# HGRN in a two-layer hybrid backbone: level 0 in one PSUM tile and one step with the product of each token with itself, and the output's products in one step

## The chip, the core and the metric

The kernel runs on one core of a Trainium2 chip. The metric is the time of one execution in device microseconds, as the median of several runs. Engines are named as the profile names them: PE is the matrix engine (PEld its weight loads), DVE the vector engine, ACT the scalar engine, POOL the GpSimd engine, SP the engine that issues most of the DMAs. Each engine takes its instructions in the order in which they were written into its queue, and waits for other engines through semaphores.

## What is computed

Two layers run over 640 tokens: 128 of context and 512 of a latent grid. Each layer projects its input to many columns, feeds four mixers with them, and merges the four results. The change is in the first mixer, HGRN2, a gated linear recurrence in both directions with 4 heads of width 128:

```python
def chunk_gla(q, k, v, log_g, s0):
    ...
    def step(S, inp):
        qc, kc, vc, gc = inp
        b = jnp.cumsum(gc, axis=2)
        diff = b[:, :, :, None, :] - b[:, :, None, :, :]
        decay = jnp.exp(jnp.where(causal[:, :, None], diff, -jnp.inf))
        attn = jnp.einsum('bhtd,bhsd,bhtsd->bhts', qc, kc, decay)
        o = (jnp.einsum('bhts,bhse->bhte', attn, vc)
             + jnp.einsum('bhtd,bhde->bhte', qc * jnp.exp(b), S))
        ...
```

The score of two tokens is their product, weakened by all gates between them. The kernel builds it by levels: level `lev` treats pairs of neighbouring blocks of 2 to the power `lev` tokens, so each pair of tokens gets its score at one level, and a token with itself (the "own" product) before level 0.

## The kernel before

Everything is held with channels on partitions and tokens along the free dimension. The input `h` is split into `h_hi` and `h_lo`, and each weight into `whi` and `wlo`, so a product takes three matmuls. One chunk of 128 projected columns (`zchunk`) has two halves of tokens, of 384 and 256 (`HALVES`), and each half 24 matmuls of L217 into one of two PSUM tiles `g`. A chunk's weights come by DMA, then ACT casts `whi` (L160), and DVE subtracts to get `wlo` (L161).

What is not a projection runs beside it in Python generators ("streams"). Before each half of a chunk the main program calls `tick()`. A stream that yields a number sleeps for that many ticks, so the code between two yields is a "step" that is written between two halves. `merge_chunk` has three ticks: two for the halves of its projection, and one before the 24 matmuls of L208 with the branch weights. The recorded program then goes through a scheduler of the language, which may put an instruction later in its engine's queue than the code does where it reckons with a wait, and sets the semaphores. It keeps track of whole tiles.

The streams that matter here:

- `hg_mix` (one for each head, two at a time at most): transposes of `v` (L514), the own product (L526) and its copy to `C` (L528), seven levels (keys `km` copied at L536, product L547, its part taken over into `C` at L549, keys, queries and gates brought on at L559 to L565), transposes of the keys (L574), states (L584), the output (L607, 13 products that PE runs as 26 instructions), its norm, and the transpose back (L620). Steps are `HG_WAIT` = 2 ticks apart, the first `HG_W0` = 3. All its PSUM tiles are `mx`, of which there are three, each two banks of 512 floats wide.
- `mods` (modulation of this layer's end and of the next layer, by DVE, ACT and POOL): 6 groups of products in layer 0 and 2 in layer 1. A group takes 14 ticks, and in 7 of them DVE (L405), ACT (L406) and POOL (L407) do one pass over 128x512 each; the sum at L410 ends it, and L417 takes the result out of PSUM. `mods` starts when the stream of head 2 has ended.
- `mla_mix` and `na_all`, the attention mixers. In `na_mix` a softmax is normed on POOL (`norm`, L929), and PE then transposes it (`TR`, L973).

In a layer the order is: the four heads' projections with the fourth mixer's, the merge of that mixer (8 `merge_chunk`s), the MLA, the merge of HGRN, neighbourhood attention, two more merges, and the output. `merge_chunk` takes its product out of PSUM on DVE (L1057 in the first merge, L1059 in the others), and the next projection needs that tile.

Of the kernel before, what the change touches and what calls it, by code (L numbers as in the profile page):

```python
# [13 lines left out]
ALU = mybir.AluOpType  # L14
# [4 lines left out]
T = 640  # L19
# [63 lines left out]
def ap_of(t, off, dims):  # L83
    base = t[:]
    return bass.AP(tensor=base.tensor, offset=base.offset + off, ap=[list(base.ap[0])] + [list(d) for d in dims])


class Build:
# [414 lines left out]
    def hg_mix(self, l, h, z, out):  # L503
        nc = self.nc
        G, RK, RQ, q, vT, sg = z
        S0 = self.u([128, 2, 128])
        nc.sync.dma_start(S0, self.I["S0"][l, h])
        ks = self.t()
        nc.vector.tensor_tensor(ks, RK[:, 0, :], RK[:, 1, :], ALU.add)
        yield HG_W0  # L510

        ps = self.mx()
        for j in range(5):
            nc.tensor.transpose(ps[:, j * 128:(j + 1) * 128], vT[:, j * 128:(j + 1) * 128], self.ident)  # L514
        v = self.t()
        nc.scalar.copy(v, ps[:, :T])


        halves = (slice(0, 64), slice(64, 128))
        five = lambda x: x[:, 0:320].rearrange("p (j t) -> p j t", j=5)  # L520

        ps = self.mx()
        for j in range(5):
            for i, r in enumerate(halves):
                sl = slice(j * 128 + 64 * i, j * 128 + 64 * i + 64)
                nc.tensor.matmul(ps[r, j * 64:(j + 1) * 64], ks[:, sl], q[:, sl], start=True, stop=True)  # L526
        C = self.t([128, 5, 64])
        nc.scalar.copy(C, five(ps))  # L528
        nc.vector.tensor_tensor(RQ[:, 0, :], q, G[:, 0, :], ALU.mult)
        nc.vector.tensor_tensor(RQ[:, 1, :], q, G[:, 1, :], ALU.mult)  # L530
        Tb, n = G, T
        for lev in range(7):
            B = 1 << lev
            np_ = T // (2 * B)
            km = self.t()
            nc.scalar.copy(km.rearrange("p (n u b) -> p n u b", u=2, b=B),  # L536
                           ap_of(RK, 0, [[2 * B, np_], [T + B, 2], [1, B]]))
            yield HG_WAIT
            ps = self.mx()
            for j in range(5):  # L540
                for i, r in enumerate(halves):
                    o = j * 128 + 64 * i
                    if B < 64:
                        x = ap_of(RQ, o, [[2 * B, 32 // B], [T + B, 2], [1, B]])
                    else:
                        x = RQ[:, 1 - i, j * 128 + 64 - 64 * i:j * 128 + 128 - 64 * i]
                    nc.tensor.matmul(ps[r, j * 64:(j + 1) * 64], km[:, o:o + 64], x, start=True, stop=True)  # L547
            if B < 64:
                nc.vector.copy_predicated(C, self.masks[:, lev:lev + 1, :].to_broadcast([128, 5, 64]), five(ps))  # L549
            else:  # L550

                A = self.t()
                Aj = A.rearrange("p (j t) -> p j t", j=5)
                for i, r in enumerate(halves):
                    nc.scalar.copy(Aj[r, :, 64 * i:64 * i + 64], C[r])
                    nc.scalar.copy(Aj[r, :, 64 - 64 * i:128 - 64 * i], five(ps)[r])

            kf = ap_of(RK, 0, [[2 * B, np_], [1, B]])
            nc.vector.tensor_tensor(kf, kf, ap_of(Tb, n + 1, [[2, np_], [0, B]]), ALU.mult)  # L559
            kb = ap_of(RK, T + B, [[2 * B, np_], [1, B]])  # L560
            nc.vector.tensor_tensor(kb, kb, ap_of(Tb, 0, [[2, np_], [0, B]]), ALU.mult)  # L561
            rq = ap_of(RQ, 0, [[2 * B, np_], [T + B, 2], [1, B]])
            nc.vector.tensor_tensor(rq, rq, ap_of(Tb, 1, [[2, np_], [n - 1, 2], [0, B]]), ALU.mult)
            T2 = self.t([128, 2, np_]) if lev == 0 else self.u([128, 2, np_])
            nc.vector.tensor_tensor(T2, ap_of(Tb, 0, [[n, 2], [2, np_]]), ap_of(Tb, 1, [[n, 2], [2, np_]]), ALU.mult)  # L565
            Tb, n = T2, np_
        yield HG_WAIT

        order = ((0, 1, 2, 3), (0, 4, 3, 2))
        ps = self.mx()  # L570
        for d in range(2):
            for i, j in enumerate(order[d]):
                o = (4 * d + i) * 128
                nc.tensor.transpose(ps[:, o:o + 128], RK[:, d, j * 128:(j + 1) * 128], self.ident)  # L574
        kt = [self.t([128, 4, 128]) for _ in range(2)]
        for d in range(2):
            nc.scalar.copy(kt[d], ps[:, 512 * d:512 * d + 512].rearrange("p (i t) -> p i t", i=4))
        yield HG_WAIT
        vv = lambda j: v[:, j * 128:(j + 1) * 128]
        ps = self.mx()  # L580
        for d in range(2):
            for i, j in enumerate(order[d]):
                o = (4 * d + i) * 128
                nc.tensor.matmul(ps[:, o:o + 128], kt[d][:, i, :], vv(j), start=True, stop=True)  # L584
        st = self.u([128, 2, 128])
        nc.scalar.copy(st, ps.rearrange("p (d i t) -> p d i t", d=2, i=4)[:, :, 0, :])
        nc.sync.dma_start(self.O["state"][l, h], st)
        S = [self.u([128, 3, 128]) for _ in range(2)]
        terms = {j: [(A[:, j * 128:(j + 1) * 128], vv(j))] for j in range(5)}
        for d in range(2):  # L590
            prev = S0[:, d, :]
            for i in range(1, 5):
                j = order[d][i] if i < 4 else (4, 1)[d]
                terms[j].append((RQ[:, 1 - d, j * 128:(j + 1) * 128], prev))
                if i < 4:
                    o = (4 * d + i) * 128
                    nc.vector.scalar_tensor_tensor(S[d][:, i - 1, :], prev, Tb[:, 1 - d, j:j + 1], ps[:, o:o + 128],
                                                   ALU.mult, ALU.add)
                    prev = S[d][:, i - 1, :]
        yield HG_WAIT  # L600

        ps = self.mx()
        for j in range(5):
            if j == 3:
                yield 1
            for i, (a, b) in enumerate(terms[j]):
                nc.tensor.matmul(ps[:, j * 128:(j + 1) * 128], a, b, start=(i == 0), stop=(i == len(terms[j]) - 1))  # L607
        sq = self.t()
        nc.scalar.activation(sq, ps[:, :T], AF.Square)
        ss = self.sm([128, 5])  # L610
        nc.vector.tensor_reduce(ss, sq.rearrange("p (j e) -> p j e", j=5), AX.X, ALU.add)
        r = self.sm([128, 5])
        self.rsqrt(r, ss, 5, 1.0 / 128, EPS)
        on = sq
        nc.vector.tensor_tensor(on.rearrange("p (j e) -> p j e", j=5), ps[:, :T].rearrange("p (j e) -> p j e", j=5),
                                r.unsqueeze(2).to_broadcast([128, 5, 128]), ALU.mult)
        yield HG_WAIT
        ps = self.mx()
        for j in range(5):
            nc.tensor.transpose(ps[:, j * 128:(j + 1) * 128], on[:, j * 128:(j + 1) * 128], self.ident)  # L620
        nc.vector.scalar_tensor_tensor(sg, ps[:, :T], self.vec("normg", l), sg, ALU.mult, ALU.mult)
        out[h] = sg
# [706 lines left out]
HG_WAIT = 2  # L1329
# [120 lines left out]
```

## Time and profile before

| what | value |
|---|---|
| runs | 2124.34 us median (2123.99 to 2128.66, three runs) |
| profiled execution | 2129.58 us, span 2127.5 us |
| PE busy | 2071.5 us (97%) |
| DVE, ACT, POOL busy | 1369.0 us (64%), 879.1 us (41%), 181.2 us (9%) |
| granted TensorE clock | 0.989 |

The profiled execution's own time is 2.1 us over its span. PE's busy time counts from an instruction's start to its end, and neighbouring matmuls overlap, so a time between two starts says more than a mean. [...]

### The profile page before, as it was taken

To read this page: it belongs to the slowest core of one execution; us is meant where nothing else is said; L and a number is where in the kernel's file an instruction comes from. 1 tells how busy PE (TensorE), PEld (TensorE's weight loads), DVE (VectorE), ACT (ScalarE), POOL (GpSimd) and SP (SyncE) were. 2 spreads that over 40 slices of the span, in tenths; PEclk is the share of its full clock that TensorE was granted. 3 is DMA by queue.
4 is the path that set the end of the run, shared out by engine and by line. 5 is a ranking of instruction groups with operands and counts; after the bars stand their busy time and mean duration, and the time that the engine had idled before them with its cause. 6 is when DMAs were issued, how large, how long until landed. Compare 5 with 4: busy or idle time off the path is not lost. (4 is left out here: it accounts for less than half of the span.)

```text
span 2127.5 us, 36907 instructions
## 1 busy us (share of the span) xinstructions
PE 2071.5 (97%) x15114; PEld 2013.0 (95%) x15114; DVE 1369.0 (64%) x2653; ACT 879.1 (41%) x1564; POOL 181.2 (9%) x156
## 2 busy tenths in 40 slices
PE   7999999999999999999999999999999999999997
PEld 4999999999999999999989999999999999999997
DVE  5677776568565667734487876873765546775456
ACT  4333334334445556523352333342443346663332
POOL 0000000111011133200010000010100002231000
PEclk9999999999999999999999999999999999999999
DMA  7222213344324411222432222143322212212251
GB/s 284 74 73 61 67 59 106 111 131 145 97 95 144 137 64 61 70 69 81 135 120 70 63 63 71 57 137 95 117 67 63 67 58 70 68 59 65 75 163 50
DMA packets 79849, 194.66 MB, mean 91 GB/s; under 512 B 9152, under 2 KB 22208, under 8 KB 79680
## 3 DMA queue, kind: packets, MB, share of 16 engines
q1 hardware_dynamic: 76656, 186.10, 27.4%
q10 hardware_dynamic: 3024, 6.20, 0.9%
q8 instruction: 119, 1.95, 0.4%
q14 instruction: 50, 0.41, 0.1%
HBM read 184.73 MB, written 7.54 MB: 90 GB/s over the span
## 5 line engine op out<-in xcount | busy, mean ns | idle before, releaser
L217 PE MATMUL g<-h_hi,whi 128*128 128x256 f32 (+1 forms) x2880 | 905.9, 315 | 16.6 <-DVE m L1057 7.0
L217 PE MATMUL g<-h_lo,whi 128*128 128x256 f32 (+1 forms) x2880 | 892.9, 310 | 0.6 <-DVE h_lo L1129 0.2
L217 PE MATMUL g<-h_hi,wlo 128*128 128x256 f32 (+1 forms) x2880 | 891.9, 310 | 0.6 <-DVE wlo L161 0.6
L217 PEld LDWEIGHTS g<-h_hi,whi 128*128 128x128 f32 x2880 | 548.1, 190 | 25.5 <-DVE m L1057 7.6
L217 PEld LDWEIGHTS g<-h_lo,whi 128*128 128x128 f32 x2880 | 548.7, 191 | 3.1 <-DVE h_lo L1129 1.6
L217 PEld LDWEIGHTS g<-h_hi,wlo 128*128 128x128 f32 x2880 | 548.1, 190 | 1.0 <-DVE wlo L161 1.0
L161 DVE TENSOR_TENSOR wlo<-wraw,whi 128x1024 fp32r<-128x1024 f32 (+1 forms) x258 | 284.1, 1101 | 281.7 <-ACT whi L160 279.5
L160 ACT CAST whi<-wraw 128x1024 fp32r<-128x1024 f32 (+1 forms) x258 | 242.8, 941 | 457.3 <-PE g L217 243.1
L208 PE MATMUL g<-t,whi 128*128 128x256 f32 (+1 forms) x1280 | 283.5, 311 | 0.7 <-ACT e L1044 0.7
L208 PEld LDWEIGHTS g<-t,whi 128*128 128x128 f32 x1280 | 214.2, 189 | 2.2 <-ACT e L1044 1.2
L208 PE MATMUL g<-t,wlo 128*128 128x384 f32 (+1 forms) x640 | 197.8, 309 | 0.0
L407 POOL TENSOR_TENSOR t<-t 128x512 f32<-128x512 f32 x56 | 82.2, 1468 | 1083.2 <-ACT t L406 1042.8
L929 POOL TENSOR_SCALAR u<-u,sm 128x320 f32<-128x320 f32 (+2 forms) x80 | 89.6, 1131 | 475.9 <-DVE sm L927 443.9
L208 PEld LDWEIGHTS g<-t,wlo 128*128 128x128 f32 x640 | 121.0, 189 | 0.0
L1044 ACT ACTIVATE e<-g,hbin 128x384 f32<-128x384 f32 (+1 forms) x128 | 67.0, 523 | 115.7 <-PE g L217 113.0
L260 ACT ACTIVATE e<-g,hbin 128x384 f32<-128x384 f32 x76 | 39.9, 525 | 97.7 <-PE g L217 80.3
L261 DVE TENSOR_SCALAR e<-g,vecs 128x384 f32<-128x384 f32 x76 | 41.3, 544 | 45.5 <-ACT e L260 45.2
L477 DVE RECIPROCAL s<-e 128x384 f32<-128x384 f32 (+1 forms) x32 | 68.8, 2149 | 0.7
L854 ACT ACTIVATE t<-mx,sm,rq 128x640 f32<-128x640 f32 (+1 forms) x40 | 31.9, 797 | 63.6 <-DVE sm L851 61.2
L536 ACT COPY t<-s 128x640 f32<-128x640 f32 x56 | 43.5, 780 | 30.4 <-DVE s L561 30.4
L405 DVE SCALAR_TENSOR_TENSOR t<-t,cf 128x512 f32<-128x512 f32 x56 | 52.7, 941 | 3.2 <-DMA t<-in_wada 1.6
L1059 DVE SCALAR_TENSOR_TENSOR e<-e,g 128x384 f32<-128x384 f32 x96 | 46.4, 484 | 12.9 <-PE g L208 12.3
(290 smaller groups left out, 2666.1 us busy)
## 6 DMA issues: line engine op xcount, KB each, us to landing
wraw<-in_win SPq DMA_DIRECT2D x184, 512.0 KB, 3.6
t<-in_wada SPq DMA_DIRECT2D x128, 256.0 KB, 4.3
wraw<-in_wbr SPq DMA_DIRECT2D x64, 256.0 KB, 2.6
wraw<-in_wout SPq DMA_DIRECT2D x20, 512.0 KB, 4.2
s<-in_wada SPq DMA_DIRECT2D x16, 512.0 KB, 7.6
s<-in_nabias SPq DMA_DIRECT2D x8, 640.0 KB, 4.9
m<-in_xT SPq DMA_DIRECT2D x8, 320.0 KB, 8.3
t<-in_xT ACTq DMA_DIRECT2D x8, 320.0 KB, 4.1
```

What stands on the lines that cost most here:

```text
L160: nc.scalar.copy(hi, raw)
L161: nc.vector.tensor_tensor(lo, raw, hi.bitcast(F32), ALU.subtract)
L208: nc.tensor.matmul(o, wsl(a, k), xsl(b, k, i), start=(k == 0 and p == 0), stop=(k == nk - 1 and p == 2))
L217: nc.tensor.matmul(ps[:, :e - a], at(u, k), v[:, k, a:e], start=(k == 0 and i == 0), stop=(k == 7 and i == 2))
L261: nc.vector.tensor_scalar(zb, ps, self.bin(l, nm, i), 0.5, ALU.add, ALU.mult)
L405: nc.vector.scalar_tensor_tensor(acc[0], raw[0], c[0], acc[0], ALU.mult, ALU.add)
L407: nc.gpsimd.tensor_tensor(acc[1], acc[1], raw[1], ALU.add)
L477: nc.vector.reciprocal(g, r)
L536: nc.scalar.copy(km.rearrange("p (n u b) -> p n u b", u=2, b=B), ap_of(RK, 0, [[2 * B, np_], [T + B, 2], [1, B]]))
L929: NORM(nc).tensor_scalar(p[e], p[e], sums[:, e:e + 1], None, ALU.mult)
L1044: self.zchunk(l, "merge", n * 8 + c, lambda ps, p, sl: nc.scalar.activation(th[p], ps, AF.Tanh, bias=hb, scale=0.5))
L1059: nc.vector.scalar_tensor_tensor(th[p], th[p], 1.0, ps, ALU.add, ALU.mult)
```

## The change

In `hg_mix` the products of queries and gates (`RQ`) and the keys of level 0 (`keys(1)`) move from the step after the first wait into the very first step. Level 0 no longer has a step and a PSUM tile of its own: its product is written into the second bank of the tile of the own product, in the same step. The output's 13 products lose the `yield 1` that stood between the third and the fourth token block. A head's stream is then shorter by 2 ticks from level 1 on, and by 3 at its end.

```diff
         ks = self.t()
         nc.vector.tensor_tensor(ks, RK[:, 0, :], RK[:, 1, :], ALU.add)
+        for d in range(2):
+            nc.vector.tensor_tensor(RQ[:, d, :], q, G[:, d, :], ALU.mult)
+
+        def keys(B):
+
+            km = self.t()
+            nc.scalar.copy(km.rearrange("p (n u b) -> p n u b", u=2, b=B),
+                           ap_of(RK, 0, [[2 * B, T // (2 * B)], [T + B, 2], [1, B]]))
+            return km
+
+        km = keys(1)
         yield HG_W0
...
-        ps = self.mx()
+        own = self.mx()
         for j in range(5):
             for i, r in enumerate(halves):
                 sl = slice(j * 128 + 64 * i, j * 128 + 64 * i + 64)
-                nc.tensor.matmul(ps[r, j * 64:(j + 1) * 64], ks[:, sl], q[:, sl], start=True, stop=True)
+                nc.tensor.matmul(own[r, j * 64:(j + 1) * 64], ks[:, sl], q[:, sl], start=True, stop=True)
         C = self.t([128, 5, 64])
-        nc.scalar.copy(C, five(ps))
-        nc.vector.tensor_tensor(RQ[:, 0, :], q, G[:, 0, :], ALU.mult)
-        nc.vector.tensor_tensor(RQ[:, 1, :], q, G[:, 1, :], ALU.mult)
+        nc.scalar.copy(C, five(own))
         Tb, n = G, T
         for lev in range(7):
             B = 1 << lev
             np_ = T // (2 * B)
-            km = self.t()
-            nc.scalar.copy(km.rearrange("p (n u b) -> p n u b", u=2, b=B),
-                           ap_of(RK, 0, [[2 * B, np_], [T + B, 2], [1, B]]))
-            yield HG_WAIT
-            ps = self.mx()
+            if lev:
+                km = keys(B)
+                yield HG_WAIT
+                ps = self.mx()
+            else:
+                ps = own[:, 512:1024]
...
         ps = self.mx()
         for j in range(5):
-            if j == 3:
-                yield 1
             for i, (a, b) in enumerate(terms[j]):
```

How many instructions each engine runs is the same. Where they stand differs. On PE, at head 1 of layer 0, the own product (L526 before, L537 after) was followed by projections alone:

```order
L547 MATMUL mx<-s,t 64x64 x10
L514 MATMUL mx<-ident,t 128x128 x5
L526 MATMUL mx<-t 64x64 x10
L217 MATMUL g<-h_hi,whi 128x256
L217 MATMUL g<-h_lo,whi 128x256
L217 MATMUL g<-h_hi,wlo 128x256
```

In the changed kernel level 0's product (L557, the second one here; the first is a level of head 0) stands 5 projection matmuls further on:

```order
L557 MATMUL mx<-s,t 64x64 x10
L525 MATMUL mx<-ident,t 128x128 x5
L537 MATMUL mx<-t 64x64 x10
L217 MATMUL g<-h_hi,whi 128x256
L217 MATMUL g<-h_lo,whi 128x256
L217 MATMUL g<-h_hi,wlo 128x256
L217 MATMUL g<-h_hi,whi 128x256
L217 MATMUL g<-h_lo,whi 128x256
L557 MATMUL mx<-s,t 64x64 x10
L217 MATMUL g<-h_hi,wlo 128x256
```

So the two products are not one run on PE: over the heads 0 to 3 of layer 0 there are 14, 5, 5 and 4 projection matmuls between them, and of layer 1 13, 5, 5 and 4. The first L557 of each head waits for the copy of the own product (L539), which reads the other bank of the same tile.

On DVE, at the beginning of neighbourhood attention of layer 0, before: the last passes of `mods` (L405) and its sum (L410) stand among the bias additions (L957), maxima (L959) and reciprocals (L927) of the first softmaxes:

```order
L405 SCALAR_TENSOR_TENSOR t<-t,cf_532 128x512
L939 TENSOR_REDUCE sm<-mx 128x2
L405 SCALAR_TENSOR_TENSOR t<-t,cf_532 128x512
L957 TENSOR_TENSOR u<-mx,s 128x192
L927 RECIPROCAL sm<-sm 128x2
L405 SCALAR_TENSOR_TENSOR t<-t,cf_532 128x512
L161 TENSOR_TENSOR wlo<-wraw,whi 128x1024
L959 TENSOR_REDUCE sm<-u 128x1
L957 TENSOR_TENSOR u<-mx,s 128x192
L405 SCALAR_TENSOR_TENSOR t<-t,cf_532 128x512
L410 TENSOR_TENSOR t<-t 128x512
L959 TENSOR_REDUCE sm<-u 128x1
```

In the changed kernel, where 8 is to be added to these line numbers, three of the four passes have moved ahead of this place and the sum stands ahead of the first bias addition:

```order
L405 SCALAR_TENSOR_TENSOR t<-t,cf_532 128x512
L947 TENSOR_REDUCE sm<-mx 128x2
L410 TENSOR_TENSOR t<-t 128x512
L965 TENSOR_TENSOR u<-mx,s 128x192
L935 RECIPROCAL sm<-sm 128x2
L967 TENSOR_REDUCE sm<-u 128x1
L965 TENSOR_TENSOR u<-mx,s 128x192
L161 TENSOR_TENSOR wlo<-wraw,whi 128x1024
L967 TENSOR_REDUCE sm<-u 128x1
```

Also on DVE, at the MLA's beginning in layer 0, before, between two rotary additions and the first softmax's maximum (L850):

```order
L660 TENSOR_TENSOR t<-t,e 128x256
L1059 SCALAR_TENSOR_TENSOR e<-e,g 128x384
L749 TENSOR_TENSOR t<-t 64x512 x2
L1060 TENSOR_TENSOR m<-m,e 128x384
L1059 SCALAR_TENSOR_TENSOR e<-e,g 128x256
L161 TENSOR_TENSOR wlo<-wraw,whi 128x1024
L405 SCALAR_TENSOR_TENSOR t<-t,cf_532 128x512
L774 TENSOR_TENSOR t<-mx,t 128x640
L1060 TENSOR_TENSOR m<-m,e 128x256
L405 SCALAR_TENSOR_TENSOR t<-t,cf_532 128x512
L850 TENSOR_REDUCE sm<-mx 128x1
```

After, the same stretch holds one pass of `mods` more, and the subtraction L757 (L749 before) stands ahead of the merge's L1067 (L1059 before):

```order
L405 SCALAR_TENSOR_TENSOR t<-t,cf_532 128x512
L668 TENSOR_TENSOR t<-t,e 128x256
L161 TENSOR_TENSOR wlo<-wraw,whi 128x1024
L757 TENSOR_TENSOR t<-t 64x512 x2
L769 TENSOR_TENSOR s<-mx,s 128x640
L1067 SCALAR_TENSOR_TENSOR e<-e,g 128x384
L405 SCALAR_TENSOR_TENSOR t<-t,cf_532 128x512
L1068 TENSOR_TENSOR m<-m,e 128x384
L161 TENSOR_TENSOR wlo<-wraw,whi 128x1024
L782 TENSOR_TENSOR t<-mx,t 128x640
L1067 SCALAR_TENSOR_TENSOR e<-e,g 128x256
L405 SCALAR_TENSOR_TENSOR t<-t,cf_532 128x512
```

Counted from its group's beginning, the last pass shown is the sixth there, where it was the third.

## Rows read from the trace of the kernel before

**Rows 1.** Windows, HGRN, layers 0 and 1: length, PE, PEld, DVE, ACT, POOL, granted clock, DMA.

```profile
60.00:364.00 304.00, 304.00 (x2467) 296.46 (x2466) 216.02 (x367) 106.82 (x164) 0.00 (x0) 1.00 0.22 69
1115.00:1413.00 298.00, 298.00 (x2431) 290.87 (x2430) 220.65 (x390) 102.44 (x157) 0.00 (x0) 1.00 0.22 68
```

**Rows 2.** Waits of PE over the span: us in total, times, longest.

```profile
PE g L217 <- DVE m L1057: 7.0, 4, 2.2
```

**Rows 3.** Windows, the merge beside mods, layers 0 and 1.

```profile
364.00:392.00 28.00, 25.15 (x203) 24.15 (x202) 26.20 (x40) 13.38 (x21) 11.21 (x7) 0.94 0.54 182
1413.00:1441.00 28.00, 23.90 (x205) 22.73 (x205) 26.22 (x41) 13.49 (x21) 11.98 (x7) 1.00 0.54 188
```

**Rows 4.** Windows, the MLA's beginning, layers 0 and 1.

```profile
484.00:530.00 46.00, 42.34 (x280) 41.60 (x279) 39.35 (x80) 21.67 (x39) 7.76 (x6) 0.96 0.52 168
1534.00:1580.00 46.00, 44.39 (x305) 43.44 (x304) 34.68 (x77) 18.31 (x33) 0.00 (x0) 1.00 0.26 77
```

**Rows 5.** Windows, neighbourhood attention's beginning, layers 0 and 1; layer 0's last part.

```profile
724.00:755.00 31.00, 24.93 (x145) 23.21 (x144) 23.98 (x40) 19.70 (x45) 13.87 (x12) 0.83 0.31 105
1768.00:1799.00 31.00, 30.11 (x214) 28.93 (x213) 21.56 (x44) 20.42 (x53) 9.03 (x9) 1.00 0.19 58
746.00:755.00 9.00, 5.80 (x32) 5.24 (x31) 5.15 (x14) 4.26 (x13) 4.94 (x5) 0.81 0.12 43
```

**Rows 6.** Waits of PE there, layer 0's longest, then layer 1's.

```profile
PE mx L973 <- POOL u L929: 3.2, 2, 2.7
...
PE mx L954 <- DVE t L921: 0.9, 1, 0.9
```

**Rows 7.** Timeline of PE: a level's block alone, then two in one (start, us).

```profile
364.68 0.34 PE L217 MATMUL g<-h_hi,wlo 128*128 128x384 f32 x1
364.94 0.85 PE L547 MATMUL mx<-s,t 128*64 128x64 f32 x20
365.95 0.28 PE L217 MATMUL g<-h_lo,whi 128*128 128x256 f32 x1
...
166.13 0.34 PE L217 MATMUL g<-h_hi,wlo 128*128 128x384 f32 x1
166.40 1.64 PE L547 MATMUL mx<-s,t 128*64 128x64 f32 x40
168.19 0.28 PE L217 MATMUL g<-h_lo,whi 128*128 128x256 f32 x1
```

**Rows 8.** Timeline of PE: ahead of an output's second step, and behind its 12 instructions.

```profile
207.52 0.28 PE L217 MATMUL g<-h_hi,wlo 128*128 128x256 f32 x1
...
209.15 0.34 PE L217 MATMUL g<-h_lo,whi 128*128 128x384 f32 x1
```

**Rows 9.** Timeline, head 2 of layer 0: own product, and the copy of it.

```profile
271.55 0.80 PE L526 MATMUL mx<-t 128*64 128x64 f32 x20
...
272.40 0.43 ACT L528 COPY t<-mx 128x320 f32<-128x320 f32 x1
```

**Rows 10.** Source L405, the whole span: ns min/median/max.

```profile
L405 DVE SCALAR_TENSOR_TENSOR t<-t,cf x56: 736/748/1780, 368.0 to 1511.7; 128x512 f32<-128x512 f32 x56
```

**Rows 11.** Timeline of DVE, then of POOL, neighbourhood attention's beginning (in brackets idle time).

```profile
746.79 0.69 DVE L410 TENSOR_TENSOR t<-t 128x512 f32<-128x512 f32 x1 [1.18 <-POOL t L407]
...
743.78 2.98 POOL L407 TENSOR_TENSOR t<-t 128x512 f32<-128x512 f32 x2 [0.97 <-ACT t L406]
```

**Rows 12.** Source L559 (ns min/median/max); then, by the timeline, one of them beside POOL.

```profile
L559 DVE TENSOR_TENSOR s<-s,u x40: 475/485/1575, 135.6 to 1432.0; 128x320 f32<-128x320 f32 x40
...
368.54 1.30 POOL L407 TENSOR_TENSOR t<-t 128x512 f32<-128x512 f32 x1 [368.12 <-ACT t L406]
368.61 1.57 DVE L559 TENSOR_TENSOR s<-s,u 128x320 f32<-128x320 f32 x1
```

**Rows 13.** Windows in layer 1: the two-column sums of the MLA, and what follows.

```profile
1519.00:1522.50 3.50, 3.50 (x34) 3.50 (x32) 0.00 (x0) 1.42 (x2) 0.00 (x0) 1.00 0.00 0
1522.90:1526.40 3.50, 3.50 (x13) 3.50 (x12) 3.13 (x14) 0.00 (x0) 0.00 (x0) 0.51 0.17 35
```

## The prediction

> **What bounds the kernel now.** I read the busy shares first. PE is busy for 97% of the span, so only two things can change the time: PE's own instructions and what they cost beside each other, and the few places where PE stands still. [...]
>
> Then I asked who makes PE wait. Of the waits in the middle of the program the largest sum is on DVE's eviction in the first merge, L1057: 7.0 us in 4 waits [rows 2]. They lie in two windows of 28 us, in which `mods` and the last head's levels run together: DVE is busy for 26.2 us of each, and PE for 25.15 and 23.90 [rows 3]. Two more places show what `mods` does, because layer 0 has it there and layer 1 does not. At the MLA's beginning PE is busy for 42.34 of 46 us in layer 0 and for 44.39 in layer 1, at clocks of 0.96 and 1.00 [rows 4]. At the beginning of neighbourhood attention it is 24.93 of 31 us against 30.11, and 0.83 against 1.00 [rows 5]. In the latter the longest wait is for POOL's norm (3.2 us in 2 waits), while layer 1 has 0.9 us in all [rows 6]. Since `mods` starts when head 2 ends, the change moves all of it three ticks ahead. That is where its effect must come from.
>
> **The change part by part.**
>
> *Level 0 beside the own product.* Products of 64 columns cost PE more than their own time when projections stand around them. A level alone: from the projection before to the second one behind 364.68 to 365.95, 1.27 us. Of this 0.29 are two usual distances of projections (0.17 and 0.12), so 0.98 is left. Two levels together: 166.13 to 168.19, less the same 0.29, is 1.77, or 0.19 less than twice 0.98 [rows 7]. One of the two is a level 0, whose columns are read with a stride and which costs 1.2 alone, so I take 0.4 us for a pair. If the own product and level 0 were one run, that would be a gain of 8 x 0.4 = 3.2 us. But the order shows 4 to 14 projections between them, so this is not won. And of the 4 pairs that levels of two heads form by chance before, 2 are left after: **+0.8 us** (bounds +0.4 and +1.0).
>
> *The output in one step.* Its 6 products of the second step run as 12 instructions. From the projection before to the second behind it is 207.52 to 209.15, 1.63 us, less 0.29 leaves 1.34 = 12 x 0.112 [rows 8]. Products of 128 columns pay nothing for standing alone, so putting the two runs together gives **0**.
>
> *The new wait.* Level 0's first product now waits for the copy of the own product. Before, the copy starts 0.05 us after the last own product ends and lands 0.48 after it: 272.35 to 272.83 [rows 9]. From the own product's end PE first needs about 0.2 us to come back to projections, and then 4 to 14 of them at 0.12 to 0.17 us, 0.5 us at the least. So the wait is just covered. I take **+0.2** (bounds 0 and +6, see the rivals). The queries and keys of level 0 are made a step earlier and were in time already.
>
> *The levels 2 ticks earlier, the end 3.* What covers them before covers them after [rows 1]: **0**.
>
> *`mods` in the first merge.* Both `mods` and head 3's levels move ahead by about one `merge_chunk`, so they stay together. DVE is filled by 94% in the window [rows 3], and the same instructions have to go through it beside the same projections. I expect the stalls at other chunks with about the same sum: **0** (bounds -3.5 and +3.5, half of the 7.0).
>
> *`mods` at the MLA's beginning, layer 0.* The order shows one pass more between the query's copy and the first maximum, where DVE has the least room. A pass takes 0.748 us in the median [rows 10], so **+0.8**. Bounds: -3.7, if all idle time went [rows 4], and +3, if the next three passes each delayed the merge's eviction as well.
>
> *`mods` at neighbourhood attention, layer 0.* Before, three passes and the group's sum stand between the first softmax's steps. The sum waits 1.18 us at the head of DVE's queue for POOL's two additions of 2.98 us, and the second maximum stands behind it [rows 11]. From it goes the chain to the norm on POOL, for which PE waits. After, only the sum and the pass before it are left, ahead of the first bias addition. Three passes are 2.2 us and the wait at the queue's head is 1.2, together 3.4, so the 3.2 us of wait [rows 6] should nearly go. With it should go the half clock in the last 9 us: 0.81 granted is 9 x 0.19 = 1.7 us [rows 5]. Of these 4.9 I take **-4.0**, since the sum still comes in between. The other waits there, 2.9 us with a clock loss of their own, belong to the preparation of keys and values, in which three passes stand before as after. They stay. Bounds: 0, and -10.5. That is the whole loss of the window in layer 0, 6.1 idle and 31 x 0.17 = 5.3 by the clock, less the 0.9 of layer 1.
>
> The sum is 0.8 + 0.2 + 0.8 - 4.0 = -2.2 us. It is made against the profiled execution, 2129.58 us, and gives 2127.4. That execution stands 5.2 us above the median of the runs, whose spread is 4.7. The clock may explain it, since it can fall with no wait at all: in layer 1 a stretch of two-column products, in which PE is busy throughout, is followed by 3.5 us at 0.51 [rows 13]. So a fall can come in one execution and not in another, at 1.7 us each, and I carry the difference over to the median: 2124.3 - 2.2 = **2122.1 us**, that is -0.1%.
>
> **The rivals.**
>
> 1. *`mods` clears the attention's preparation too.* For it: the bound of -10.5; DVE gets past its backlog sooner when four passes are gone from the stretch. Against it: the three passes in the preparation are the same in number. It would give some -6 in place of -4, and with one stall of the first merge gone (-2) 2124.3 + 1.8 - 8 = 2118, down to 2114.5 if all goes.
>
> 2. *Nothing comes out.* The wait for POOL's norm goes, but what is late next is the preparation's keys or the next softmax, which takes most of it back. For it: DVE is busy for 24 of the 31 us. Then it is 2124.3 + 1.8 - 1 = 2125.
>
> 3. *Slower by the new wait.* Place: the first product of level 0 of heads 1 to 3 in both layers, six times, with 4 or 5 projections as cover. If one or two other instructions go ahead of the copy on ACT (164 take 106.82 us there, 0.65 each [rows 1]), it lands 1.1 to 1.8 us after the own product's end, and PE stands still for about 0.8 us each time, 5 us in all: 2122 + 5 = 2127, and 2130 where the clock falls behind it. It decides from where the copy lands later than about 0.7 us after the own product. Against it: before, ACT took the copy 0.05 us after the own product [rows 9], and it has the same instructions to do around it.
>
> 4. *DVE is slowed down by POOL elsewhere.* A multiplication at L559 takes 0.485 us in the median and 1.575 at most; one of the slowest runs beside one of POOL's additions, 368.61 beside 368.54 to 369.84 [rows 12]. A shift of `mods` picks other victims. If two more in each layer come ahead of an eviction in the first merge, PE waits for 4 x 1.1 = 4.4 us: 2126.5. [...]
>
> That the change does not do what its words say is so in part: level 0 is one step with the own product in the code but not one run on PE. That stands in the sum.
>
> **How the numbers follow.** A measurement of this kernel tells about 0.2% (4.2 us) from no change: the three runs lie 0.2% apart. Chances: the forecast (2119.5 to 2124) 0.42; rival 1 (2114.5 to 2119.5) 0.23; rival 2 (2124 to 2127) 0.15; rival 3 0.11; rival 4 0.09. Faster by over 0.2% means below 2120.1: rival 1 and a quarter of the forecast, 0.34. Slower means above 2128.6: half of rivals 3 and 4 and a clock that falls more often, 0.14. The rest is 0.52. The range is 2114.5 to 2129.
>
> **What would show each step.** Right: the wait at L1057 keeps a sum of 5 to 9 us; the wait of the second transpose on POOL's norm in layer 0 falls below 1 us, and the clock of the last part of that window is 1.00; the waits at the MLA's beginning come to 4 or 5 us; level 0's products wait for less than 0.5 us in all; the HGRN windows stay without idle time. Wrong: any wait at the first level-0 products of over 0.3 us, waits at L1057 below 4 or above 10 us, or a stall of the attention that merely moved to the next transpose. One thing would upset the carrying over to the median: if the half clock after the two-column products came in one kernel's runs alone.

## The result: 0.56% slower

Before took 2126.16 us (median of six runs, 2123.99 to 2128.66), the changed kernel 2137.40 (six runs, 2133.99 to 2140.40). The ratio is 1.0056, with a 95% interval from 1.0045 to 1.0066. The forecast was 2122.1, with a range up to 2129: the time lies outside, on the slower side. The profiled execution of after took 2137.39 us, span 2135.6, granted clock 0.988.

### The profile after

Most line numbers are 8 higher now. Waits of PE over the span: us in total, times, longest.

```profile
PE g L217 <- DVE e L1067: 7.1, 5, 3.7
PE g L217 <- DVE m L1065: 6.8, 6, 2.6
...
PE g L208 <- ACT e L1052: 4.6, 6, 1.5
PE mx L791 <- ACT u L771: 4.3, 1, 4.3
...
PE mx L981 <- POOL u L937: 0.8, 3, 0.3
```

The first merge's wait (L1065, which was L1057) has the sum it had in [rows 2]. POOL's norm (L937) is down to 0.8 over the span; in neighbourhood attention of layer 0 it was 3.2 [rows 6], and is 0.2. New are 3.7 us for the eviction L1067 and 4.3 for L771, a copy of MLA keys. No level 0 is in the list.

Windows of after: length, PE, PEld, DVE, ACT, POOL, granted clock, DMA.

```profile
60.00:366.00 306.00, 305.77 (x2488) 297.44 (x2488) 222.69 (x381) 109.87 (x169) 4.47 (x3) 1.00 0.24 73
1118.00:1416.00 298.00, 297.18 (x2437) 289.13 (x2436) 223.58 (x401) 104.24 (x160) 2.79 (x2) 1.00 0.23 72
364.00:392.00 28.00, 25.70 (x215) 24.59 (x214) 21.48 (x31) 9.94 (x16) 8.10 (x5) 1.00 0.41 134
418.00:446.00 28.00, 25.36 (x181) 25.16 (x180) 18.63 (x33) 9.41 (x14) 6.40 (x5) 0.97 0.44 141
...
486.00:534.00 48.00, 39.79 (x243) 38.62 (x243) 40.44 (x71) 22.23 (x38) 9.01 (x7) 0.89 0.42 139
...
1776.00:1807.00 31.00, 30.12 (x214) 28.95 (x213) 21.55 (x44) 20.44 (x53) 8.91 (x8) 1.00 0.20 58
756.00:768.00 12.00, 12.00 (x86) 11.60 (x85) 8.14 (x20) 7.68 (x20) 6.74 (x6) 1.00 0.21 70
```

PE is still busy almost throughout the heads, 305.77 of 306 and 297.18 of 298 us at a granted clock of 1.00, as in [rows 1]. The part of the attention that had 0.81 of the clock [rows 5] has 1.00 and no idle time (the last row). The MLA's beginning has got worse: 8.2 us idle in 48 and a clock of 0.89, against 3.7 idle and 0.96 in [rows 4].

Where the time went is read most safely by taking the same projection (the same L217 matmul, counted from the first) in both traces. Counted from 0, the marks are numbers 0, 1608, 2280 and 2616, then 3288 and 3456, then 4296, 4560, 6576 and 6912. Between seven pairs of them it took, in us (each a difference of two starts):

| stretch | before | after | difference |
|---|---|---|---|
| heads 0 to 2, layer 0 | 287.7 | 289.2 | +1.5 |
| head 3 and first merge, layer 0 | 154.9 | 157.1 | +2.2 |
| MLA's beginning, layer 0 | 96.6 | 105.1 | **+8.5** |
| neighbourhood attention's beginning, layer 0 | 48.1 | 42.7 | **-5.4** |
| layer 0's end | 121.4 | 117.0 | -4.4 |
| heads and first merge, layer 1 | 386.9 | 388.9 | +2.0 |
| MLA's beginning, layer 1 | 75.0 | 78.7 | **+3.7** |

With the rest, which is equal within 0.1, this makes +8.1 us. Layer 0's end has nothing to do with the change: before's profiled execution took 121.4 there, with a granted clock of 0.51 from 1028 to 1035 us, and the other fifteen kernels of this study 116.6 to 119.9. Without it the profiles differ by +12.5, and the medians by 11.2.

The heads' own stretches have become longer, by nearly the same amount in every kernel with both parts. From number 480 to number 1608 it is 199.8 us in layer 0 of the three kernels with the old heads (before, and e4 and e13 of the experiments below), and 201.3 in the eight with both parts (after, e3, e5 to e8, e11 and e12). The same stretch of layer 1 (4896 to 6024) takes 200.4 and 202.6 to 202.9. So the change costs 1.5 and at least 2.2 us there, and in after only 0.6 of that is idle time of PE.

### The two long waits

PE at the MLA's beginning (start, us, in brackets the idle time before and what ended it):

```profile
473.66 0.95 PE L414 MATMUL mx<-e,t 128*128 128x2 f32 x8
474.47 2.37 PE L688 MATMUL mx<-ones,t 128*128 128x2 f32 x20
476.71 1.26 PE L691 MATMUL mx<-ones,t 128*128 128x2 f32 x10
...
478.48 0.52 PE L217 MATMUL g<-h_hi,whi 128*128 128x384 f32 x1
...
483.66 0.28 PE L217 MATMUL g<-h_hi,whi 128*128 128x256 f32 x1
...
501.96 0.45 PE L217 MATMUL g<-h_hi,whi 128*128 128x384 f32 x1 [3.67 <-DVE e L1067]
...
502.53 0.52 PE L217 MATMUL g<-h_hi,wlo 128*128 128x384 f32 x1
```

```profile
524.71 0.80 PE L791 MATMUL mx<-u 128*128 128x128 f32 x2 [4.29 <-ACT u L771]
```

L791 waits for ACT's copy L771, and that for DVE's subtraction L769. So DVE was late; ACT had been idle (2.13 us ahead of L771). DVE and then POOL ahead of it:

```profile
511.21 0.28 DVE L739 COPY u<-mx 128x128 f32<-128x128 f32 x1
511.41 1.63 DVE L405 SCALAR_TENSOR_TENSOR t<-t,cf 128x512 f32<-128x512 f32 x1
512.97 1.31 DVE L749 COPY u<-t 128x128 f32<-128x128 f32 x1
...
514.62 2.71 DVE L666 TENSOR_TENSOR e<-t,cs 32x256 f32<-32x256 f32 x4
...
518.14 1.71 DVE L666 TENSOR_TENSOR e<-t,cs 32x256 f32<-32x256 f32 x4
519.88 0.75 DVE L405 SCALAR_TENSOR_TENSOR t<-t,cf 128x512 f32<-128x512 f32 x1
...
523.53 0.82 DVE L769 TENSOR_TENSOR s<-mx,s 128x640 fp32r<-128x640 f32 x1
```

```profile
511.20 1.29 POOL L407 TENSOR_TENSOR t<-t 128x512 f32<-128x512 f32 x1 [15.07 <-ACT t L406]
512.67 3.09 POOL L407 TENSOR_TENSOR t<-t 128x512 f32<-128x512 f32 x2 [0.18 <-ACT t L406]
```

The same instructions appear twice on DVE: L405 with 1.63 us beside POOL and 0.75 alone, four L666 with 2.71 and 1.71. The copy L749 takes 1.31 us and 0.23 in the median. So three additions on POOL cost DVE 0.9 + 1.1 + 1.0 = 3.0 us, beside the 1.5 us of the two passes L405 themselves. The first wait arises in the same way: ahead of L1067 stand a pass, and two L666 that take 1.86 beside POOL and 0.84 alone.

In layer 0, of the 8.5 us, the wait at L1067 is 2.5 (3.67 now, 1.15 before), half clock behind it 1.6 (0.54 granted from 501.96 to 505.50), the waits up to L791 and behind it 1.8 (4.29 now; 0.42 and 2.08 before). 1.6 is half clock behind the two-column products, where 24 matmuls take 477.82 to 483.66, 5.84 us at 0.71 of the clock and not 4.28 at 1.00. That leaves 1.0, to which the longer half clock behind the second wait belongs (0.54 granted in the 5.29 us from L791 on; in before 0.68 in as many behind the wait of 2.08).

The 1.6 us behind the two-column products are not the work of `mods`. The same 24 matmuls take 5.55 to 6.89 us in fourteen of the sixteen traces, among them those in which `mods` starts where it did and no L414 stands ahead of the sums; only before and e12 have 4.28. In e3, below, it is 5.86 us:

```profile
470.20 0.43 PE L217 MATMUL g<-h_hi,whi 128*128 128x384 f32 x1
...
476.06 0.28 PE L217 MATMUL g<-h_hi,whi 128*128 128x256 f32 x1
```

So here the profile of before had luck, and against e3, which has the same fall, the MLA's beginning of after is 9.6 us longer.

### The profile page after: what moved, and what is told of

It is laid out like the page before. It is cut to its first block, busy times and chain, and to the rows that moved or that the text cites. A ratio compares the mean times of both kernels' runs of the same rounds, so it can differ in the third digit from the quotient of the medians.

```text
span 2135.6 us, 36888 instructions
## 1 busy us (share of the span) xinstructions
PE 2075.8 (97%) x15114; PEld 2014.8 (94%) x15114; DVE 1368.2 (64%) x2653; ACT 878.8 (41%) x1564; POOL 181.3 (8%) x156
## 5 line engine op out<-in xcount | busy, mean ns | idle before, releaser
L217 PE MATMUL g<-h_hi,whi 128*128 128x256 f32 (+1 forms) x2880 | 906.2, 315 | 18.1 <-DVE e L1067 7.1
L217 PE MATMUL g<-h_lo,whi 128*128 128x256 f32 (+1 forms) x2880 | 894.4, 311 | 0.3
L217 PE MATMUL g<-h_hi,wlo 128*128 128x256 f32 (+1 forms) x2880 | 893.6, 310 | 0.6 <-DVE wlo L161 0.6
L217 PEld LDWEIGHTS g<-h_hi,whi 128*128 128x128 f32 x2880 | 549.1, 191 | 26.8 <-DVE m L1065 7.9
L217 PEld LDWEIGHTS g<-h_lo,whi 128*128 128x128 f32 x2880 | 549.4, 191 | 2.9 <-DVE h_lo L432 1.2
L217 PEld LDWEIGHTS g<-h_hi,wlo 128*128 128x128 f32 x2880 | 549.0, 191 | 1.6 <-DVE wlo L161 1.0
L208 PE MATMUL g<-t,whi 128*128 128x256 f32 (+1 forms) x1280 | 283.6, 311 | 4.6 <-ACT e L1052 4.6
L208 PEld LDWEIGHTS g<-t,whi 128*128 128x128 f32 x1280 | 214.1, 189 | 7.2 <-ACT e L1052 6.4
L208 PE MATMUL g<-t,wlo 128*128 128x384 f32 (+1 forms) x640 | 197.8, 309 | 0.0
L407 POOL TENSOR_TENSOR t<-t 128x512 f32<-128x512 f32 x56 | 82.7, 1477 | 1079.4 <-ACT t L406 1030.8
L937 POOL TENSOR_SCALAR u<-u,sm 128x320 f32<-128x320 f32 (+2 forms) x80 | 89.2, 1127 | 492.4 <-PE mx L962 285.4
L208 PEld LDWEIGHTS g<-t,wlo 128*128 128x128 f32 x640 | 121.0, 189 | 0.0
L405 DVE SCALAR_TENSOR_TENSOR t<-t,cf 128x512 f32<-128x512 f32 x56 | 56.6, 1010 | 10.6 <-DMA t<-in_wada 8.3
L1067 DVE SCALAR_TENSOR_TENSOR e<-e,g 128x384 f32<-128x384 f32 x96 | 46.3, 483 | 12.7 <-PE g L208 12.2
```

Of the source, the lines that this page charges most:

```text
L208: nc.tensor.matmul(o, wsl(a, k), xsl(b, k, i), start=(k == 0 and p == 0), stop=(k == nk - 1 and p == 2))
L217: nc.tensor.matmul(ps[:, :e - a], at(u, k), v[:, k, a:e], start=(k == 0 and i == 0), stop=(k == 7 and i == 2))
L405: nc.vector.scalar_tensor_tensor(acc[0], raw[0], c[0], acc[0], ALU.mult, ALU.add)
L407: nc.gpsimd.tensor_tensor(acc[1], acc[1], raw[1], ALU.add)
L937: NORM(nc).tensor_scalar(p[e], p[e], sums[:, e:e + 1], None, ALU.mult)
L1067: nc.vector.scalar_tensor_tensor(th[p], th[p], 1.0, ps, ALU.add, ALU.mult)
```

## The experiments

Theory A: the loss comes from `mods`, which starts 3 ticks earlier. Theory B: from head 3's end, which now falls into the first merge's last chunk. Theory C: from level 0's step itself. What speaks for B is a wait of 2.64 us that is new:

```profile
443.42 0.44 PE L217 MATMUL g<-h_hi,whi 128*128 128x384 f32 x1 [2.64 <-DVE m L1065]
```

Ahead of that eviction DVE had head 3's norm together with three passes, and POOL's additions beside them:

```profile
434.07 1.28 DVE L195 SCALAR_TENSOR_TENSOR sm<-sm 128x5 f32<-128x5 f32 x1
...
436.19 4.78 DVE L405 SCALAR_TENSOR_TENSOR t<-t,cf 128x512 f32<-128x512 f32 x3
...
442.82 0.87 DVE L1065 SCALAR_TENSOR_TENSOR m<-e,g 128x384 f32<-128x384 f32 x2
```

```profile
434.03 1.29 POOL L407 TENSOR_TENSOR t<-t 128x512 f32<-128x512 f32 x1 [15.29 <-ACT t L406]
435.72 3.00 POOL L407 TENSOR_TENSOR t<-t 128x512 f32<-128x512 f32 x2 [0.40 <-ACT t L406]
```

All experiments, in medians; the ratio is to the kernel before on the same chip. "Start" is that of `mods` in ticks against before.

| run | heads | start | us | ratio (95%) | MLA, layer 0 | MLA, layer 1 | attention, layer 0 |
|---|---|---|---|---|---|---|---|
| before | before | 0 | 2126.2 | | 96.6 | 75.0 | 48.1 |
| after | both parts | -3 | 2137.4 | 1.0056 (1.0045 to 1.0066) | 105.1 | 78.7 | 42.7 |
| e1 | level 0 | -2 | 2128.4 | 1.0011 (1.0001 to 1.0020) | 99.2 | 74.3 | 46.5 |
| e2 | output | -1 | 2134.9 | 1.0044 (1.0031 to 1.0057) | 98.0 | 75.0 | 45.1 |
| e3 | both | 0 | 2122.6 | 0.9980 (0.9969 to 0.9991) | 95.5 | 74.9 | 48.1 |
| e4 | before | -3 | 2134.6 | 1.0038 (1.0025 to 1.0052) | 104.3 | 78.4 | 42.7 |
| e5 | both, head 3 late | -3 | 2135.7 | 1.0044 (1.0030 to 1.0058) | 105.2 | 77.4 | 42.7 |
| e9 | level 0 | 0 | 2121.8 | 0.9982 (0.9973 to 0.9990) | 95.4 | 75.7 | 48.0 |
| e10 | output | 0 | 2133.1 | 1.0029 (1.0017 to 1.0041) | 97.4 | 75.0 | 48.1 |
| e11 | both | +3 | 2116.5 | 0.9960 (0.9947 to 0.9973) | 95.9 | 75.3 | 39.1 |
| e12 | both | +9 | 2147.4 | 1.0094 (1.0080 to 1.0108) | 106.0 | 86.0 | 38.1 |
| e13 | before | +3 | 2118.8 | 0.9968 (0.9955 to 0.9980) | 96.9 | 75.4 | 39.2 |
| e14 | level 0 | +3 | 2117.4 | 0.9967 (0.9954 to 0.9980) | 96.0 | 75.3 | 39.1 |

The last three columns are the stretches of the table above. They follow the start of `mods` whatever the heads are: 95.4 to 97.4 at 0, 104.3 to 105.2 at -3, and likewise in the attention.

**e1 and e2: one part alone.** e1 is the changed kernel with the output's `yield` put back, e2 the kernel before with it taken out:

```diff
         for j in range(5):
-            if j == 3:
-                yield 1
```

> Level 0's part alone: the output keeps its two steps. Heads end 2 ticks earlier than in the kernel before, and `mods` starts 2 ticks earlier. Theory A (the loss is `mods`, which starts earlier and meets the MLA's beginning): some 2130 to 2137 us, with a loss of 6 to 10 us between 490 and 565 us of the span. Theory B (head 3's end, which falls into the last chunk of the first merge): the norm moves by 2 of the 3 ticks, 2128 to 2133, with the loss between 430 and 470. Theory C (level 0's step itself, its tile and its wait): the whole loss, 2137, spread over the heads.

> The output's products in one step alone: level 0 keeps its own step and tile. Heads end 1 tick earlier, `mods` starts 1 tick earlier. Theory A: between nothing and a third of the loss, 2124 to 2130 us. Theory B: the same, but with the difference between 430 and 470 us of the span. Theory C: 2126, as the kernel before.

The two medians add up to after's loss (2.2 and 8.7 us, against 11.2), but place by place they don't, so that is chance, and no theory gave both sizes. At the MLA in layer 0 they cost 2.6 and 1.4 us where after has 8.5, in the first merge of layer 0 -1.6 and +7.4 where after has +2.2. Most of e2's loss lies in the merges, and e10 comes back to it.

**e3 and e4: `mods` moved without the heads, and the heads without `mods`.** In e3 `mods` waits 3 ticks more. In e4, whose lines stand 1 or 2 higher than in before, it starts when head 2 comes to its output (its stream notes that in `self.near`).

```diff
 e3   while self.busy(after):
          yield 1
+     yield 3
 e4   while self.busy(after)
+         and (todo[0][0], 2) not in self.near
```

> The changed kernel, with `mods` delayed by 3 ticks, so that it starts where it did in the kernel before, while the heads still end earlier. Theory A: the wait of 4.3 us for the keys' copy and most of that of 3.7 us on the eviction L1067 go, and with them half clock, some 10 us; the 5 us won at neighbourhood attention are lost again: 2137.4 - 10 + 5 = 2132 us. Theories B and C: nothing comes back, and the attention's gain is lost: 2140 to 2143.

> The kernel before, with nothing changed in the heads, but `mods` starts 3 ticks earlier: where head 2's output begins, not where its stream ends. Theory A: the MLA's loss of 10 us and the attention's gain of 5 alone, 2126.2 + 5 = 2131 us. Theories B and C: only the attention's gain, 2121.

e3 gives all back and is 0.2% faster than before, more than theory A expected: the attention does lose its 5.4 us, but the first merge wins as well (150.5 us where after has 157.1). PE in e3, where after waits 3.67, and in e4:

```profile
491.94 0.44 PE L217 MATMUL g<-h_hi,whi 128*128 128x384 f32 x1 [0.87 <-DVE e L1067]
```

```profile
500.81 0.69 PE L218 MATMUL g<-h_hi,whi 128*128 128x384 f32 x1 [3.65 <-DVE e L1061]
...
523.39 0.38 PE L785 MATMUL mx<-u 128*128 128x128 f32 x1 [4.29 <-ACT u L765]
```

With heads that nobody touched, e4 has both waits to within 0.02 us, and 8.4 of after's 11.2 us. It is 3.6 us slower than theory A had it, since the first merge loses too (2.5 us in layer 0). Theory C is out: nothing of level 0 is in e4, and all of it is in e3.

**e5: head 3's end put back.** Its output waits `HG_WAIT + 3` in the changed kernel.

> The changed kernel, with head 3 alone waiting 3 ticks longer ahead of its output; `mods` starts as early as in the changed kernel. Theory B's part: head 3's norm no longer falls into the last chunk of the first merge, so the wait of 2.64 us at 443 us goes, and half clock of 3.4 us behind it (1.7 us), in layer 1 the 0.46 and 0.89 us: 2137.4 - 5 = 2132 us. The waits of 3.67 and 4.29 us at the MLA's beginning stay, if `mods` alone makes them; if head 3's end has a part in them, they fall by over 1 us.

The wait at 443 us is gone and the first merge takes 3.1 us less, with a new wait of 1.30 at L642. The MLA's waits stay (3.65 and 4.29). The median moves by 1.7 us and not the 5 expected, less than the intervals can tell. So theory B's part in the time is small, if it has one.

**e6 and e7: what of `mods` does it.** e6 leaves out L407 on POOL, e7 the passes L405 on DVE.

```diff
 e6  -  nc.gpsimd.tensor_tensor(acc[1], acc[1], raw[1], ALU.add)
 e7  -  nc.vector.scalar_tensor_tensor(acc[0], raw[0], c[0], acc[0], ALU.mult, ALU.add)
```

> The changed kernel without POOL's additions L407: half of each product of `mods` is left out of the sum. Theory P (POOL slows DVE's work beside it): the wait of 4.29 us for the keys' copy falls by the slowing of L405, L749 and L666 beside POOL, 0.9 + 1.0 + 1.0 = 2.9 us, to 1.4, that of 3.67 on L1067 by 1 us; with the half clock 2128 to 2132 us. Theory D (the passes themselves fill DVE): both waits stay over 3 us, 2135 to 2137.

> The changed kernel without DVE's passes L405: the other half of each product of `mods` is left out but for its first pass, POOL's and ACT's stay. Theory D: the two waits at the MLA's beginning fall to 1 us or less, the first merge loses its waits, 2115 to 2122 us. Theory P: the wait on L1067 falls by the one pass ahead of it, 0.75, that for the keys' copy by two, 1.5 us, since POOL's additions then slow other work: 2124 to 2130.

They took 2116.9 us (ratio 0.9960, 0.9948 to 0.9973) and 2121.4 (0.9981, 0.9972 to 0.9991). e6 is 11 us below both theories' ranges, and e7 is in theory D's: neither theory had priced the first merge, whose stretch of layer 0 falls from 157.1 to 149.1 and 150.0 us. So the theories are judged by the waits. Without POOL, PE's two waits (lines are 1 lower), and the pass L405 over the span (ns, min/median/max):

```profile
494.16 0.44 PE L217 MATMUL g<-h_hi,whi 128*128 128x384 f32 x1 [2.66 <-DVE e L1066]
...
513.95 0.38 PE L790 MATMUL mx<-u 128*128 128x128 f32 x1 [1.30 <-ACT u L770]
```

```profile
L405 DVE SCALAR_TENSOR_TENSOR t<-t,cf x56: 740/745/753, 357.9 to 1487.1; 128x512 f32<-128x512 f32 x56
```

The keys' wait falls from 4.29 to 1.30 as theory P had it to 0.1 us, and no L405 is slow any more. Without DVE's passes:

```profile
494.95 0.60 PE L217 MATMUL g<-h_hi,whi 128*128 128x384 f32 x1 [3.00 <-DVE e L1066]
...
516.56 0.45 PE L217 MATMUL g<-h_hi,whi 128*128 128x384 f32 x1 [2.29 <-DVE e L1066]
```

Of the wait of 3.67, the pass ahead of it is 0.67 (theory P: 0.75) and POOL's slowing 1.01. If the two add up, which no run shows, about 2.0 would be left without both, where before had 1.15 with them; what makes up that 0.85 is open. The keys' wait of 4.29 is gone in e7, and the next one is the 2.29 for an eviction, so its share for the passes can't be read off. At the MLA's beginning in layer 0 POOL's additions account for 4.5 us and the passes for 3.2. So neither theory holds alone.

**e8: thinner.** One pass every second tick (`yield 2` in the loop).

> The changed kernel with one pass of `mods` every second tick instead of every tick, so that DVE gets half as many passes beside a chunk and the whole of it lasts about 1.6 times as long. If the loss comes from passes crowded at a few places, the first merge's waits (3.3 us and the 2.64 at 443) and the MLA's fall below half: 2118 to 2126 us. If each pass costs wherever it stands, the time stays at 2133 to 2138.

It took 2132.0 us (1.0030, 1.0019 to 1.0042), between the two ranges. The first merge got better (149.8 us) and the MLA's beginning was 99.7. But `mods` then lasted through the whole neighbourhood attention, whose norms need POOL, and the stretch behind its beginning grew from 209.6 to 221.9 us.

**e9 and e10: each part with `mods` where it was.**

> Level 0's part alone, with `mods` delayed by 2 ticks, so that it starts where it did in the kernel before. What level 0's step itself is worth: the pairs of 64-column blocks cost 1 to 2 us in the heads; the earlier ends of the heads relieve the first merge. If the merge's relief in the run with `mods` 3 ticks late comes from levels that end earlier, it shows here too: 2121 to 2125 us. If it comes from the output's single step, 2126 to 2129.

> The output's part alone, with `mods` delayed by 1 tick. If the loss of 8.7 us of that part came from `mods` starting a tick earlier, it goes: 2123 to 2127 us. If it came from the head's own end (waits of 5.4 us in sum on the norm ahead of the last transposes), half of it or more stays: 2129 to 2133.

Level 0 alone is as fast as both parts (e3). That both are faster than before by 0.2%, clear of noise, shows what the heads are worth with `mods` in its old place: they lose in their own stretches and win more in the first merge (154.9 us in before, 150.5 in e3, 151.3 in e9). The output alone keeps a loss of 7 us, and there the forecast had "0". In e10 head 3's norm on DVE, and what PE then waits for:

```profile
441.45 1.25 DVE L194 TENSOR_TENSOR sm<-sm 128x5 f32<-128x5 f32 x1
...
443.28 1.22 DVE L195 SCALAR_TENSOR_TENSOR sm<-sm 128x5 f32<-128x5 f32 x1
```

```profile
445.51 0.74 PE L618 MATMUL mx<-ident,t 128*128 128x128 f32 x5 [2.52 <-DVE t L613]
```

In before one step of this norm is held up beside POOL (L193, 1.25 us at 445.04, with an addition from 444.89 to 446.27), and PE does not wait for it. One tick earlier, in e10, two of the steps take that long, 1.25 and 1.22 us, where 0.17 is usual. Over the span L618 makes PE wait for 6.4 us. That POOL holds these two as well is concluded from their length alone.

**e11 to e14: where `mods` is best.** The delay of e3 with 6 and 12 ticks; the kernel before with 3; level 0's part alone with 5.

> The changed kernel with `mods` delayed by 6 ticks, 3 later than in the kernel before. If each tick later takes `mods` further out of the way of the first merge and the MLA's beginning, 2114 to 2122 us. If the time depends on which step of `mods` meets which step of the merge and the MLA, without a direction, it lies anywhere from 2118 to 2138, and the waits stand at other places than with 3 ticks.

> The changed kernel with `mods` delayed by 12 ticks, nearly a whole group (15 ticks). The same two theories as with 6 ticks: 2110 to 2120 us if later is better throughout; if the step that is met decides, then near the kernel with `mods` early (2137), since a group of 15 ticks and 12 ticks of delay bring nearly the same steps to the same places one group later.

> The kernel before, with nothing changed in the heads, and `mods` starting 3 ticks later, at the same place as in the changed kernel delayed by 6 ticks. If that kernel's 2116.5 us come from the place of `mods` alone, this one is as fast, 2115 to 2118 us, and the change in the heads is worth nothing. If the heads have a part of their own, as the run with `mods` 3 ticks late suggests (3.6 us below the kernel before), it stands 3 to 5 us above: 2119 to 2122.

> Level 0's part alone, with `mods` delayed by 5 ticks, at the same place again. If the output's single step is worth nothing or costs a little (0.9 us between the two runs with `mods` kept), 2114 to 2118 us, within 2 us of the changed kernel delayed by 6 ticks.

e11 is 10 us faster than before. In the first window, in the first merge, PE has no wait (0.3 us over the whole merge), and the MLA's beginning has the full clock:

```profile
364.00:392.00 28.00, 28.00 (x248) 26.96 (x247) 15.17 (x22) 10.51 (x17) 4.79 (x3) 1.00 0.50 159
486.00:534.00 48.00, 46.30 (x316) 45.02 (x315) 38.04 (x79) 24.49 (x43) 6.40 (x5) 1.00 0.40 124
```

e12 shows that later is not better as such. Its `mods` starts 12 ticks later than in after, nearly a group (14 ticks; the expectation says 15). Nearly the same steps meet the MLA again, now in both layers. Layer 1 loses 11 us as well, and the time is 10 us above the 2137 expected:

```profile
492.39 0.69 PE L217 MATMUL g<-h_hi,whi 128*128 128x384 f32 x1 [3.79 <-DVE e L1067]
...
516.11 0.58 PE L791 MATMUL mx<-u 128*128 128x128 f32 x1 [4.05 <-ACT u L771]
```

```profile
1548.85 0.69 PE L217 MATMUL g<-h_hi,whi 128*128 128x384 f32 x1 [3.79 <-DVE e L1067]
...
1571.76 0.38 PE L791 MATMUL mx<-u 128*128 128x128 f32 x1 [4.05 <-ACT u L771]
```

And e13, with the heads as they were, stands 2.3 us above e11, between the two expectations and with overlapping intervals: at this place of `mods`, the change in the heads is worth nothing that can be measured. Elsewhere it is worth something else. With the same start of `mods`, the changed heads make -3.6 us at 0 (e3 against before) and +2.8 at -3 (after against e4, where the intervals overlap).

## Why the prediction was wrong

- **The step that failed is "`mods` at the MLA's beginning, layer 0": +0.8, at most +3.** It measured +8.5 (+7.7 in e4, where nothing else is changed). The order did show the one pass more, and the forecast priced it as one pass of DVE. It left out two things. A group's step also brings additions on POOL, and these held up work of DVE beside them (e6: 4.5 us here). And DVE had no room there, so PE waited, 3.67 and 4.29 us, and its clock fell behind each wait (0.54 granted in the next 3.54 and 5.29 us). Of the 8.5 us, 1.6 are the fall behind the two-column sums that before's profile happened not to have. The mechanism stood in the text as rival 4, with the right size for one victim (1.1 us), but with its place in the first merge and a chance of 0.09.
- **The MLA in layer 1 had no term.** It measured +3.7. The window of [rows 4] shows POOL idle there, from which nothing was asked of `mods`. But the end of its second group reaches it: 30 sums take 5.05 us there (1524.77 to 1529.82) at 0.65 of the clock, where they took 3.27 at 1.00. In layer 1 the sums take 3.58 to 5.11 us in the five kernels that have L414 directly ahead of them, and 3.27 in the others (3.63 in e8). That is 1.8 of the 3.7 us. Nearly all of the rest are waits of PE for casts and evictions on ACT at the MLA's products L208, 3.1 us where before had 0.7 and another 0.9 for DVE; they are in e4 and e5 too and not in e3, and what leads from `mods` to them is open.
- **"`mods` in the first merge": 0, within 3.5.** In after its wait has the old sum (6.8 us), as foreseen. But the argument, that `mods` and head 3 move together and so nothing changes, is wrong. They do stay together, but the merge's chunks don't move with them: an eviction of its last chunk now stands behind the norm and the passes (2.64 us). And `mods` alone moved by 3 ticks (e4) costs 2.5 and 1.2 us in the two stretches with the first merge. That after's 2.2 us in layer 0 lie inside the bounds is luck: with the new heads the move of `mods` costs 6.6 us there (157.1, against 150.5 in e3), and the heads win 4.3 back.
- **"`mods` at neighbourhood attention": -4.0.** Right: -5.4, the wait on POOL's norm there down from 3.2 to 0.2, the clock of the last part 1.00.
- **"The new wait": +0.2.** Right, it is nil. Head 2 of layer 0: the copy L539 on ACT ends at 273.18, level 0 (L557) starts at 273.42.

```profile
272.75 0.43 ACT L539 COPY t<-mx 128x320 f32<-128x320 f32 x1
```

```profile
273.42 0.80 PE L557 MATMUL mx<-s,t 128*64 128x64 f32 x14
```

- **"Level 0 beside the own product": +0.8.** Right in sign, too small. With level 0's part alone (e1 and e9, numbers 480 to 1608 and 4896 to 6024) heads 0 to 2 cost 2.0 us more in each layer, 2.3 in e9's layer 1. How much of that is pairs lost, and how much other places of the levels among the projections, is open.
- **"The output in one step": 0.** Nearly right for the heads (0.4 us more in each layer, e2 and e10). But the tick that is saved isn't free, since it moves the norm (e10).
- **Carrying over to the median.** The 2124.3 came from three runs; six gave 2126.16, which is 1.8 of the 15.3 us by which the forecast missed. That a fall of the clock puts the profile above the median fits layer 0's end, 4.4 us longer than in after (0.51 granted from 1028 to 1035 us).

## What to carry over

A stream that starts when another ends moves with every tick that is saved in that other one, so its whole collision with the work beside it has to be priced again, place by place, in all layers; here the move of 3 ticks was worth 8.4 us with the old heads (e4) and 14.8 with the new (after against e3), and the change of the heads between -3.6 and +2.8, depending on where that stream stood. The price of a background step is what all its engines do to the bottleneck's feeders: here a pass on DVE (0.75 us), plus the time for which POOL's additions hold DVE up (0.9 to 1.1 us each), plus the clock behind each wait (1.6 us behind that of 3.67). Where such a stream has slack, make its start a number of its own and sweep it: here +3 ticks won 0.3% with nothing else changed (e13).

## What was not expected of the hardware

L195 and the passes L405, where one of POOL's additions held them up, were not slowed in proportion: they ended only after the addition had. L195, 0.166 us in the median, took 1.28: it started at 434.07, POOL's addition ran from 434.03 to 435.32, and L195 ended at 435.35. So it took the 1.25 us that were left of the addition, short as it is by itself. Of the 24 passes L405 that start during an addition, the two that start in its last 0.10 us keep their length. The other 22 end 0.55 or 0.56 us after the addition does, and take 0.92 to 1.82 us for it, where 0.75 is usual. Not every instruction is held: the copy L739 at 511.21, beside an addition from 511.20 to 512.49, took its usual 0.28 us, and the eight evictions L1065 that start during an addition are no longer than the others (0.41 to 0.54 us, where all 32 take 0.41 to 0.56). Both read a PSUM tile; whether that is why, no run shows.

The granted clock also fell while PE never stood still. In layer 1 of after PE ran 38 products of two columns, the 8 of `mods` and the 30 sums:

```profile
1522.00:1526.00 4.00, 4.00 (x38) 4.00 (x36) 0.60 (x4) 1.42 (x2) 0.00 (x0) 1.00 0.08 27
1526.00:1530.00 4.00, 4.00 (x22) 4.00 (x22) 0.01 (x1) 0.00 (x0) 0.00 (x0) 0.53 0.01 4
1530.00:1534.00 4.00, 4.00 (x15) 4.00 (x16) 3.56 (x17) 0.00 (x0) 0.00 (x0) 0.61 0.28 68
```

In layer 1 of before the fall came only behind the sums, with 0.51 [rows 13]; here it comes among them. The 8 products of `mods` do not seem to be needed for that: in layer 0 of e11 30 sums alone take 4.36 us (464.97 to 469.33) and not 3.27, which a fall would explain. In layer 0 of before it did not fall at all: 1.00 from 470 to 477 us. What decides it is open.
